# Second SwiGLU layer of an encoder block: weight sums of a Strassen pair formed by adding DMA loads, and one product in another PSUM pool

## Chip, cores and metric

One core of a Trainium2 chip. The metric is the device time of one execution in microseconds; several executions are timed and their median is given.

## The reference

One residual block on x (512 tokens, 1024 features), float32: a half-step SwiGLU layer, a token mixer (gated DeltaNet and latent attention), and a second half-step SwiGLU layer, each behind an adaptive RMS norm. Only the second SwiGLU layer matters here:

```python
def _swiglu(h, w_in, w_out):                    # h 512x1024, w_in 1024x5632, w_out 2816x1024
    gate, up = jnp.split(h @ w_in, 2, axis=-1)
    return (jax.nn.silu(gate) * up) @ w_out
x = x + 0.5 * g3[:, None, :] * _swiglu(_modulate(x, sh3, s3), ffn2_w_in[l], ffn2_w_out[l])
```

## The kernel before

Activations are kept feature-major, in tiles of 128 features by 512 tokens. Each float32 operand is split into a high part (a cast to fp32r on ScalarE) and a low part (a subtract on VectorE), and a product is made of three matmuls: high by high, high by low, low by high.

The 2816 hidden features of the second layer are 22 blocks of 128, each with a gate block `g` and an up block `u` of the weights (1024 rows, loaded as one tile of 128 x 1024, 512 KB). The first four blocks (eight "units", 0 to 7) are multiplied plainly. The other 18 are "pairs": `g` and `u` of one block, each halved along the 1024 rows (A and B), with the tokens halved too, form a 2x2 matrix product that a Strassen scheme computes with seven products instead of eight. It needs four sums of weight halves: gA + gB, uA + gA, and two more made of these. `pair_tasks` makes the sums, splits all weights and handles the results; `product` makes the seven products (`up0`, `up1`, `s2`, `s3`, `s1`, `s4`, `gate1`), each of 12 matmuls of 256 columns. `token_sums` makes the sums on the token side, T(0) to T(7).

**Order.** `ffn2_rest` writes the order of the layer out by hand, and `in_order` pins it: on every engine, and on SyncE's queue of loads, the instructions run in the order in which the program emits them. The loop runs over ticks s; pair j has base 7j, and its products stand at base + 0, 1, 3, 4, 6, 9 and 12 (`STEPS`). The list in `pair_tasks` says at which tick, counted from the base, a task is emitted: the load at -11, the sums at -7 and -5, the splits from -6 to 0, and then the copies, sums and SiLUs of the results. Between the products, `fill` places the matmuls of the down projection (`down`, four blocks at a time, whose weights are cast four ticks and subtracted three ticks before use, and `finish`, line 868, which adds a result tile to x). For ticks 24 to 38 there are almost no fills.

**The entry.** Before tick 0, the list `steps` interleaves units 3 to 7, the token sums, the first SwiGLU results (`glu`) and the tasks of pair 0. An entry that is a generator is run to its first `yield`, and its second half is run after the first half of the next one; a tuple is run at once. Pair 0's tasks at base + 0 and earlier stand in `steps` and not in the tick list. Pair 1's load stands in `steps` and in the tick list as well.

**Buffers.** Raw weights go to pool `wp` with tag `wr`, four buffers of 512 KB, shared by units, pairs and down weights; a load waits until a buffer's last reader is done. High and low parts have four buffers each (`wh`, `wl`). The sums have one buffer each in `ws` (`sx` and `sy`). The two PSUM pools are `psa` (three banks, taken with `acc`) and `psb` (five banks, taken with `aux`). Units 0 to 2 are accumulated in the three banks of `psa` before the entry; products 3 to 7 take their banks in `products`.

In the profile a tile's name is that of its variable or tag: `sx` and `sy` are the sums, `gh`/`gl` the parts of gB, `yh`/`yl` those of the tile `y`, `pa` and `pb` the banks of `psa` and `psb`. GpSimd (POOL) has no work in the second layer.

Of the kernel before, what the change touches and what calls it, by code (L numbers as in the profile page):

```python
# [11 lines left out]
F32 = mybir.dt.float32  # L12
# [3 lines left out]
ALU = mybir.AluOpType  # L16
AX = mybir.AxisListType

P = 128
NT = 512  # L20
# [3 lines left out]
DFF = 2816  # L24
# [55 lines left out]
class Block:  # L80
# [656 lines left out]
    def pair_tasks(self, f, base, add):  # L737


        nc, v, w = self.nc, self.nc.vector, self.ins["ffn2_w_in"][0]  # L740
        r = {}
        flat = lambda t: t.rearrange("p k f -> p (k f)")
        A, B = slice(0, NT), slice(NT, 2 * NT)

        def tiles(names, tags, dt, bufs):
            for n, tag in zip(names, tags):
                r[n] = self.ws.tile([P, 2 * NT], dt, tag=tag, name=self.name(tag), bufs=bufs)

        def load():
            for n, c in (("g", f * P), ("u", DFF + f * P)):  # L750
                t = self.wp.tile([P, 8, P], F32, tag="wr", name=self.name("wr"))
                self.load(t, w[:, c:c + P].rearrange("(k p) f -> p k f", p=P))
                r[n] = flat(t)

        def sums():
            tiles(("x", "y"), ("sx", "sy"), F32, 1)
            v.tensor_tensor(out=r["y"][:, A], in0=r["g"][:, A], in1=r["g"][:, B], op=ALU.add)
            v.tensor_tensor(out=r["x"][:, A], in0=r["u"][:, A], in1=r["g"][:, A], op=ALU.add)

        def sums2():  # L760
            v.scalar_tensor_tensor(out=r["x"][:, B], in0=r["y"][:, A], scalar=-1.0, in1=r["u"][:, A], op0=ALU.mult,
                                   op1=ALU.subtract)
            v.tensor_tensor(out=r["y"][:, B], in0=r["u"][:, B], in1=r["x"][:, B], op=ALU.subtract)

        def hi(name, src, part=slice(0, 2 * NT)):
            def go():
                if name == "g1":
                    r["g1h"], r["g1l"] = self.slot(F32R, "gh"), self.slot(F32R, "gl")
                elif name == "y":
                    tiles(("yh", "yl"), ("yh", "yl"), F32R, 2)  # L770
                else:
                    for e in "hl":
                        r[name + e] = flat(self.wp.tile([P, 8, P], F32R, tag="w" + e, name=self.name("w" + e)))
                nc.scalar.copy(r[name + "h"], r[src][:, part])
            return go

        def lo(name, src, part=slice(0, 2 * NT)):
            def go():
                v.tensor_tensor(out=r[name + "l"], in0=r[src][:, part], in1=r[name + "h"].bitcast(F32), op=ALU.subtract)
            return go  # L780

        def early_copy(name, part):
            def go():
                if name not in r:
                    r[name] = self.slot(s=name)
                nc.scalar.copy(r[name][:, part], r["A"][:, :HALF])
            return go

        L, H = slice(0, HALF), slice(HALF, NT)

        def both():
            v.tensor_tensor(out=r["cc"], in0=r["cc"], in1=r["BC"], op=ALU.add)

        def gate0():
            v.tensor_tensor(out=r["uc"][:, H], in0=r["uc"][:, L], in1=r["BC"][:, H], op=ALU.add)
            nc.scalar.activation(r["uc"][:, H], r["uc"][:, H], AF.Silu, scale=-1.0)

        def gate1():
            nc.scalar.activation(r["cc"][:, H], r["cc"][:, H], AF.Silu, scale=-1.0)

        def act1():
            v.tensor_tensor(out=r["cc"][:, H], in0=r["cc"][:, H], in1=r["A"][:, :HALF], op=ALU.mult)

        def act0():
            v.tensor_tensor(out=r["cc"][:, L], in0=r["cc"][:, L], in1=r["uc"][:, H], op=ALU.mult)
            r["ah"] = self.slot(F32R, "ah")
            nc.scalar.copy(r["ah"], r["cc"])

        def act_low():
            al = self.slot(F32R, "al")  # L810
            v.tensor_tensor(out=al, in0=r["cc"], in1=r["ah"].bitcast(F32), op=ALU.subtract)
            self.act.append((r["ah"], al))

        r["do"] = dict(load=load, sums=sums, sums2=sums2)
        for n, src, part in (("u", "u", slice(0, 2 * NT)), ("x", "x", slice(0, 2 * NT)), ("y", "y", slice(0, 2 * NT)), ("g1", "g", B)):
            r["do"][n] = hi(n, src, part), lo(n, src, part)
        for at, go in ((-11, load), (-7, sums), (-5, sums2), (-6, hi("u", "u")), (-4, lo("u", "u")), (-4, hi("x", "x")),
                       (-3, lo("x", "x")), (-3, hi("y", "y")), (-2, lo("y", "y")), (-1, hi("g1", "g", B)),
                       (0, lo("g1", "g", B)), (1, early_copy("cc", L)), (4, early_copy("uc", L)), (7, early_copy("cc", H)),
                       (8, both), (9, gate1), (11, act1), (13, gate0), (15, act0), (16, act_low)):  # L820
            if base > 0 or at > 0:
                add(base + at, go)
        return r

    def product(self, r, what):


        if "A" not in r:
            r["A"], r["BC"] = self.aux(), self.aux()
        L, H = slice(0, HALF), slice(HALF, NT)  # L830
        b = lambda k0, ts: [(self.h[k][0][:, ts], self.h[k][1][:, ts]) for k in range(k0, k0 + 4)]
        out, w, part, xs, start, stop = {
            "up0": (r["A"][:, L], "u", 0, b(0, L), True, False), "up1": (r["BC"][:, L], "u", 1, b(4, L), True, True),
            "s2": (r["A"][:, L], "x", 1, self.T["t2"], False, False), "s3": (r["BC"][:, H], "x", 0, self.T["t3"], True, False),
            "s1": (r["A"][:, L], "y", 0, self.T["t1"], False, False), "s4": (r["A"][:, L], "y", 1, b(4, H), False, True),
            "gate1": (r["BC"][:, H], "g1", 0, self.T["t4"], False, True)}[what]
        mm, kw = self.nc.tensor.matmul, dict(skip_group_check=True)
        for k, (xh, xl) in enumerate(xs):
            c = slice(part * NT + k * P, part * NT + k * P + P)
            wh, wl = r[w + "h"][:, c], r[w + "l"][:, c]  # L840
            mm(out, wh, xh, start=start and k == 0, stop=False, **kw)  # L841
            mm(out, wh, xl, start=False, stop=False, **kw)  # L842
            mm(out, wl, xh, start=False, stop=stop and k == 3, **kw)  # L843

    def ffn2_rest(self, ps):

        nc = self.nc
# [10 lines left out]
        n = FT - PLAIN  # L858
# [50 lines left out]
        d0 = down(0, 4, 1, 1.3)  # L909
# [12 lines left out]
        raws, split, accs = {}, {3: self.next_unit(ahead=0)}, {0: ps[0], 1: ps[1], 2: ps[2]}  # L922

        def unit_split(i):
            hi, lo = (self.wp.tile([P, 8, P], F32R, tag=t, name=self.name(t)) for t in ("wh", "wl"))
            nc.scalar.copy(hi, raws[i])
            split[i] = hi, lo
            yield
            nc.vector.tensor_tensor(out=lo, in0=raws[i], in1=hi.bitcast(F32), op=ALU.subtract)  # L929

        def glu(f):
            s = self.slot(s="sg")
            nc.scalar.activation(s, accs[2 * f], AF.Silu)
            a = self.slot(s="af")
            nc.vector.tensor_tensor(out=a, in0=s, in1=accs[2 * f + 1], op=ALU.mult)
            ah, al = self.slot(F32R, "ah"), self.slot(F32R, "al")
            nc.scalar.copy(ah, a)
            self.act.append((ah, al))
            yield
            nc.vector.tensor_tensor(out=al, in0=a, in1=ah.bitcast(F32), op=ALU.subtract)  # L940

        def products(i):
            accs[i] = self.acc()
            self.dense(accs[i], split[i], self.h)

        def of(go):
            if isinstance(go, tuple):
                go[0]()
                yield
                go[1]()  # L950
            else:
                go()
# [2 lines left out]
        T = lambda i: self.token_sums(i % 4, i // 4)  # L955
        for i in (4, 5, 6, 7):
            raws[i] = raw(i)
        steps = [unit_split(4), T(0), T(1), glu(0), (products, 3), T(2), (do["load"],), unit_split(5), T(3), (products, 4),
                 glu(1), T(4), unit_split(6), T(5), (products, 5), of(do["sums"]), of(do["sums2"]), unit_split(7), (d0[0],),
                 glu(2), (products, 6), T(6), of(do["u"]), of(do["x"]), (do1["load"],), T(7), of(do["y"]), of(tuple(d0[1:])),  # L960
                 (products, 7), glu(3), of(do["g1"])]
        waiting = None
        for g in steps:
            if isinstance(g, tuple):
# [8 lines left out]
        k0, m = 16, 6  # L973
# [1127 lines left out]
```

## Time and profile before

| | us |
|---|---|
| timed executions | 1081.54, 1086.86, 1089.51 (median 1086.86) |
| profiled execution, whole | 1081.86 |
| its span in the trace | 1080.1 |
| PE busy in the span | 1046.8 (97%) |
| VectorE busy | 698.7 (65%) |
| ScalarE busy | 436.8 (40%) |
| GpSimd busy | 43.3 (4%) |
| first matmul of product 3 (entry) | 739.77 |
| first matmul of pair 0 | 768.71 |

The trace's times count from the start of the span, and 1.8 us of the execution lie around it. A row of the timeline has start, duration, engine, line, operation, the tile written and the tiles read, shape, count, and in brackets how long the engine was idle before it and what released it. PE's rows overlap, since matmuls are pipelined; the distance from one start to the next is the time that each takes.

### The profile page before, as it was taken

To read this page: it belongs to the slowest core of one execution; us is meant where nothing else is said; L and a number is where in the kernel's file an instruction comes from. 1 tells how busy PE (TensorE), PEld (TensorE's weight loads), DVE (VectorE), ACT (ScalarE), POOL (GpSimd) and SP (SyncE) were. 2 spreads that over 40 slices of the span, in tenths; PEclk is the share of its full clock that TensorE was granted. 3 is DMA by queue.
4 is the path that set the end of the run, shared out by engine and by line. 5 is a ranking of instruction groups with operands and counts; after the bars stand their busy time and mean duration, and the time that the engine had idled before them with its cause. 6 is when DMAs were issued, how large, how long until landed. Compare 5 with 4: busy or idle time off the path is not lost. (4 is left out here: it accounts for less than half of the span.)

```text
span 1080.1 us, 15643 instructions
## 1 busy us (share of the span) xinstructions
PE 1046.8 (97%) x6183; PEld 897.7 (83%) x6183; DVE 698.7 (65%) x1240; ACT 436.8 (40%) x752; POOL 43.3 (4%) x94
## 2 busy tenths in 40 slices
PE   6999999999999999998999899998999999999998
PEld 4778878788887899886777678987899999999997
DVE  4488984333587456468867645787768877777633
ACT  4242222222222345475574443454434444444322
POOL 1000000000000010102000030200000000000000
PEclk9999999999999999999999889999999999999999
DMA  9989973332687345211213001121532433333222
GB/s 274 274 250 299 288 217 98 98 98 88 212 289 235 108 127 165 76 39 40 79 34 89 20 21 40 39 79 59 156 116 74 123 104 99 93 117 98 65 73 78
DMA packets 204471, 133.18 MB, mean 123 GB/s; under 512 B 13665, under 2 KB 188526, under 8 KB 204398
## 3 DMA queue, kind: packets, MB, share of 16 engines
q1 hardware_dynamic: 204398, 132.18, 41.4%
q8 instruction: 48, 0.79, 0.3%
q14 instruction: 25, 0.20, 0.1%
HBM read 129.67 MB, written 2.49 MB: 122 GB/s over the span
## 5 line engine op out<-in xcount | busy, mean ns | idle before, releaser
L262 PE MATMUL pa<-hh,wh 128*128 128x512 f32 (+1 forms) x605 | 230.5, 381 | 8.4 <-ACT z L1916 4.3
L263 PE MATMUL pa<-hl,wh 128*128 128x512 f32 (+1 forms) x605 | 228.6, 378 | 3.5 <-DVE hl L449 3.3
L264 PE MATMUL pa<-hh,wl 128*128 128x512 f32 (+1 forms) x605 | 227.8, 377 | 0.0
L193 ACT CAST wh<-wr 128x1024 fp32r<-128x1024 f32 (+1 forms) x106 | 107.7, 1018 | 253.9 <-PE pa L263 177.6
L194 DVE TENSOR_TENSOR wl<-wr,wh 128x1024 fp32r<-128x1024 f32 (+1 forms) x106 | 125.1, 1181 | 101.9 <-ACT wh L193 99.5
L262 PE MATMUL pa<-ah,wh 128*128 128x512 f32 (+1 forms) x396 | 145.5, 367 | 0.5 <-DVE xT L868 0.4
L263 PE MATMUL pa<-al,wh 128*128 128x512 f32 (+1 forms) x396 | 144.5, 365 | 0.0
L264 PE MATMUL pa<-ah,wl 128*128 128x512 f32 (+1 forms) x396 | 143.5, 362 | 0.0
L262 PEld LDWEIGHTS pa<-hh,wh 128*128 128x128 f32 x605 | 114.6, 190 | 32.7 <-ACT z L1916 4.7
L263 PEld LDWEIGHTS pa<-hl,wh 128*128 128x128 f32 x605 | 114.6, 189 | 24.1 <-DVE hl L449 4.8
L264 PEld LDWEIGHTS pa<-hh,wl 128*128 128x128 f32 x605 | 114.7, 190 | 20.2 <-DVE wl L194 0.4
L264 PEld LDWEIGHTS pa<-ah,wl 128*128 128x128 f32 x396 | 74.8, 189 | 12.0
L262 PEld LDWEIGHTS pa<-ah,wh 128*128 128x128 f32 x396 | 75.2, 190 | 10.4 <-ACT wh L193 1.7
L547 DVE SCALAR_TENSOR_TENSOR aa<-ar,sc,aa 128x512 f32<-128x512 f32 x98 | 73.0, 748 | 13.1 <-DMA ar<-in_w_ada 11.6
L263 PEld LDWEIGHTS pa<-al,wh 128*128 128x128 f32 x396 | 75.2, 190 | 7.2
L841 PE MATMUL pb<-fh,wh 128*128 128x256 f32 x144 | 40.7, 283 | 0.0
L868 DVE SCALAR_TENSOR_TENSOR xT<-pa,mod,xT 128x512 f32<-128x512 f32 (+1 forms) x40 | 29.4, 736 | 17.6 <-PE pa L264 17.6
L843 PE MATMUL pb<-fh,wl 128*128 128x256 f32 x144 | 40.7, 283 | 0.0
L843 PE MATMUL pb<-hh,wl 128*128 128x256 f32 x144 | 40.7, 283 | 0.0
L842 PE MATMUL pb<-fl,wh 128*128 128x256 f32 x144 | 40.7, 282 | 0.0
L842 PE MATMUL pb<-hl,wh 128*128 128x256 f32 x144 | 40.7, 282 | 0.0
L841 PE MATMUL pb<-hh,wh 128*128 128x256 f32 x144 | 40.6, 282 | 0.0
(430 smaller groups left out, 1956.5 us busy)
## 6 DMA issues: line engine op xcount, KB each, us to landing
wr<-in_ffn_w_in SPq DMA_DIRECT2D x84, 512.0 KB, 3.9
ar<-in_w_ada SPq DMA_DIRECT2D x48, 512.0 KB, 6.9
wr<-in_ffn_w_out SPq DMA_DIRECT2D x34, 512.0 KB, 4.1
ar<-in_w_ada SPq DMA_DIRECT2D x48, 256.0 KB, 4.2
wr<-in_w_in SPq DMA_DIRECT2D x21, 512.0 KB, 3.9
wr<-in_ffn_w_out SPq DMA_DIRECT2D x17, 384.0 KB, 3.5
wr<-in_w_out SPq DMA_DIRECT2D x8, 512.0 KB, 4.6
wr<-in_ffn_w_in SPq DMA_DIRECT2D x8, 384.0 KB, 7.2
```

The source lines that it names most:

```text
L193: self.nc.scalar.copy(hi, raw)
L194: self.nc.vector.tensor_tensor(out=lo, in0=raw, in1=hi.bitcast(F32), op=ALU.subtract)
L262: mm(out, wh, xh, start=start, stop=False)
L263: mm(out, wh, xl, start=False, stop=False)
L264: mm(out, wl, xh, start=False, stop=stop)
L547: nc.vector.scalar_tensor_tensor(out=acc, in0=a, scalar=sc, in1=acc, op0=ALU.mult, op1=ALU.add)
L841: mm(out, wh, xh, start=start and k == 0, stop=False, **kw)
L842: mm(out, wh, xl, start=False, stop=False, **kw)
L843: mm(out, wl, xh, start=False, stop=stop and k == 3, **kw)
L868: nc.vector.scalar_tensor_tensor(out=self.xT[t][:, ts], in0=p[:, ts], scalar=gate[:, t:t + 1], in1=self.xT[t][:, ts], op0=ALU.mult, op1=AL ...
```

## The change

Two of the four weight sums of each pair are no longer made on VectorE. Before, `sums` made gA + gB in `y` and uA + gA in `x` with two VectorE instructions. Now SyncE loads uA a second time into `x`, and GpSimd issues two loads with `accum_op=ALU.add`: gA is added to `x`, and gB is added to the A half of `g`, which then holds gA + gB beside gB and takes the place of `y`. The fourth sum, in `sums3`, overwrites uA in the tile `u`. So the tile `sy` is gone and `sx` has two buffers; products `s4` and `gate1` swap which split weights they read; the load moves to tick -10, the sums to -9, and the other tasks by a tick or so. `x` and `u` are split from their tiles as before, `y` from `g`, and `g1` from the A half of `u`.

In the entry, product 3 takes its bank from `psb` (`aux`) instead of `psa`, T(0) to T(2) stand ahead of the split of unit 4, and the tasks of pairs 0 and 1 are placed anew. Pair 1's first two tasks are left out of the tick list, so that its load is emitted once.

```diff
@@ -746,21 +746,27 @@
             for n, tag in zip(names, tags):
                 r[n] = self.ws.tile([P, 2 * NT], dt, tag=tag, name=self.name(tag), bufs=bufs)
 
+        rows = lambda c, k0, n: w[k0 * P:(k0 + n) * P, c:c + P].rearrange("(k p) f -> p k f", p=P)
+        cg, cu = f * P, DFF + f * P
+
         def load():
-            for n, c in (("g", f * P), ("u", DFF + f * P)):
+            tiles(("x",), ("sx",), F32, 2)
+            for n, c in (("g", cg), ("u", cu)):
                 t = self.wp.tile([P, 8, P], F32, tag="wr", name=self.name("wr"))
-                self.load(t, w[:, c:c + P].rearrange("(k p) f -> p k f", p=P))
+                self.load(t, rows(c, 0, 8))
                 r[n] = flat(t)
+            self.load(r["x"][:, A].rearrange("p (k f) -> p k f", k=4), rows(cu, 0, 4))
 
         def sums():
-            tiles(("x", "y"), ("sx", "sy"), F32, 1)
-            v.tensor_tensor(out=r["y"][:, A], in0=r["g"][:, A], in1=r["g"][:, B], op=ALU.add)
-            v.tensor_tensor(out=r["x"][:, A], in0=r["u"][:, A], in1=r["g"][:, A], op=ALU.add)
+            for n, k0 in (("x", 0), ("g", 4)):
+                nc.gpsimd.dma_start(r[n][:, A].rearrange("p (k f) -> p k f", k=4), rows(cg, k0, 4), accum_op=ALU.add)
 
         def sums2():
-            v.scalar_tensor_tensor(out=r["x"][:, B], in0=r["y"][:, A], scalar=-1.0, in1=r["u"][:, A], op0=ALU.mult,
+            v.scalar_tensor_tensor(out=r["x"][:, B], in0=r["g"][:, A], scalar=-1.0, in1=r["u"][:, A], op0=ALU.mult,
                                    op1=ALU.subtract)
-            v.tensor_tensor(out=r["y"][:, B], in0=r["u"][:, B], in1=r["x"][:, B], op=ALU.subtract)
+
+        def sums3():
+            v.tensor_tensor(out=r["u"][:, A], in0=r["u"][:, B], in1=r["x"][:, B], op=ALU.subtract)
 
         def hi(name, src, part=slice(0, 2 * NT)):
             def go():
@@ -811,14 +817,15 @@
             v.tensor_tensor(out=al, in0=r["cc"], in1=r["ah"].bitcast(F32), op=ALU.subtract)
             self.act.append((r["ah"], al))
 
-        r["do"] = dict(load=load, sums=sums, sums2=sums2)
-        for n, src, part in (("u", "u", slice(0, 2 * NT)), ("x", "x", slice(0, 2 * NT)), ("y", "y", slice(0, 2 * NT)), ("g1", "g", B)):
+        r["do"] = dict(load=load, sums=sums, sums2=sums2, sums3=sums3)
+        for n, src, part in (("u", "u", slice(0, 2 * NT)), ("x", "x", slice(0, 2 * NT)), ("y", "g", slice(0, 2 * NT)), ("g1", "u", A)):
             r["do"][n] = hi(n, src, part), lo(n, src, part)
-        for at, go in ((-11, load), (-7, sums), (-5, sums2), (-6, hi("u", "u")), (-4, lo("u", "u")), (-4, hi("x", "x")),
-                       (-3, lo("x", "x")), (-3, hi("y", "y")), (-2, lo("y", "y")), (-1, hi("g1", "g", B)),
-                       (0, lo("g1", "g", B)), (1, early_copy("cc", L)), (4, early_copy("uc", L)), (7, early_copy("cc", H)),
-                       (8, both), (9, gate1), (11, act1), (13, gate0), (15, act0), (16, act_low)):
-            if base > 0 or at > 0:
+        for i, (at, go) in enumerate(((-10, load), (-9, sums), (-5, hi("u", "u")), (-4, lo("u", "u")), (-4, sums2), (-3, hi("x", "x")), (-3, sums3),
+                       (-2, lo("x", "x")), (-1, hi("y", "g")), (0, lo("y", "g")), (0, hi("g1", "u", A)),
+                       (1, lo("g1", "u", A)), (1, early_copy("cc", L)), (4, early_copy("uc", L)), (7, early_copy("cc", H)),
+                       (8, both), (9, gate1), (11, act1), (13, gate0), (15, act0), (16, act_low))):
+            by_hand = 12 if base == 0 else 2 if base == 7 else 0
+            if i >= by_hand:
                 add(base + at, go)
         return r
 
@@ -832,8 +839,8 @@
         out, w, part, xs, start, stop = {
             "up0": (r["A"][:, L], "u", 0, b(0, L), True, False), "up1": (r["BC"][:, L], "u", 1, b(4, L), True, True),
             "s2": (r["A"][:, L], "x", 1, self.T["t2"], False, False), "s3": (r["BC"][:, H], "x", 0, self.T["t3"], True, False),
-            "s1": (r["A"][:, L], "y", 0, self.T["t1"], False, False), "s4": (r["A"][:, L], "y", 1, b(4, H), False, True),
-            "gate1": (r["BC"][:, H], "g1", 0, self.T["t4"], False, True)}[what]
+            "s1": (r["A"][:, L], "y", 0, self.T["t1"], False, False), "s4": (r["A"][:, L], "g1", 0, b(4, H), False, True),
+            "gate1": (r["BC"][:, H], "y", 1, self.T["t4"], False, True)}[what]
         mm, kw = self.nc.tensor.matmul, dict(skip_group_check=True)
         for k, (xh, xl) in enumerate(xs):
             c = slice(part * NT + k * P, part * NT + k * P + P)
@@ -940,7 +947,7 @@
             nc.vector.tensor_tensor(out=al, in0=a, in1=ah.bitcast(F32), op=ALU.subtract)
 
         def products(i):
-            accs[i] = self.acc()
+            accs[i] = self.aux() if i == 3 else self.acc()
             self.dense(accs[i], split[i], self.h)
 
         def of(go):
@@ -955,10 +962,10 @@
         T = lambda i: self.token_sums(i % 4, i // 4)
         for i in (4, 5, 6, 7):
             raws[i] = raw(i)
-        steps = [unit_split(4), T(0), T(1), glu(0), (products, 3), T(2), (do["load"],), unit_split(5), T(3), (products, 4),
-                 glu(1), T(4), unit_split(6), T(5), (products, 5), of(do["sums"]), of(do["sums2"]), unit_split(7), (d0[0],),
-                 glu(2), (products, 6), T(6), of(do["u"]), of(do["x"]), (do1["load"],), T(7), of(do["y"]), of(tuple(d0[1:])),
-                 (products, 7), glu(3), of(do["g1"])]
+        steps = [T(0), T(1), T(2), unit_split(4), glu(0), (products, 3), T(3), unit_split(5), (do["load"],), (do["sums"],), (products, 4), T(4),
+                 glu(1), unit_split(6), T(5), (products, 5), unit_split(7), (d0[0],), of(do["sums2"]), T(6),
+                 of(do["u"]), glu(2), of(do["sums3"]), (products, 6), of(do["x"]), (do1["load"],), (do1["sums"],), T(7), of(do["y"]),
+                 of(tuple(d0[1:])), (products, 7), glu(3), of(do["g1"])]
         waiting = None
         for g in steps:
             if isinstance(g, tuple):
```

## Prediction

> **What bounds the kernel now.** I read the page's busy shares first, then busy time by stage over the second FFN, then the PE timeline around the one hole that the stages show, then VectorE, ScalarE and SyncE over one steady pair.
>
> ```profile
> PE 1046.8 (97%) x6183; PEld 897.7 (83%) x6183; DVE 698.7 (65%) x1240; ACT 436.8 (40%) x752; POOL 43.3 (4%) x94
> 736.00:740.00 4.00, 0.34 (x2) 0.23 (x2) 2.90 (x5) 2.03 (x4) 0.00 (x0) 1.00 0.23 68
> 740.00:744.00 4.00, 4.00 (x12) 3.13 (x12) 3.84 (x8) 2.19 (x3) 0.00 (x0) 0.57 0.21 63
> 744.00:764.00 20.00, 20.00 (x90) 16.55 (x89) 15.22 (x25) 8.53 (x12) 0.00 (x0) 1.00 0.27 80
> 838.00:1040.00 202.00, 201.96 (x1404) 188.52 (x1403) 146.31 (x203) 87.00 (x144) 0.00 (x0) 1.00 0.34 100
> ```
>
> The columns after the stretch are its length, busy time (and count) of PE, PEld, DVE, ACT and POOL, granted clock, DMA share and GB/s. In the loop over pairs (838 to 1040) PE is busy 201.96 of 202 us, DVE 146.31 and POOL not at all. So VectorE work taken away there is worth nothing by itself: PE's matmuls hide it. The hole is the entry, 736 to 740, and the stretch behind it runs at a granted clock of 0.57.
>
> ```profile
> 735.83 0.28 PE L264 MATMUL pa<-hh,wl 128*128 128x256 f32 x1
> 739.77 0.57 PE L262 MATMUL pa<-hh,wh 128*128 128x512 f32 x1 [3.66 <-ACT sg L933]
> 740.13 0.63 PE L263 MATMUL pa<-hl,wh 128*128 128x512 f32 x1
> 750.35 0.39 PE L262 MATMUL pa<-hh,wh 128*128 128x512 f32 x1
> 750.58 0.39 PE L263 MATMUL pa<-hl,wh 128*128 128x512 f32 x1
> 738.60 0.62 ACT L733 CAST fh<-tv 128x512 fp32r<-128x512 f32 x1 [1.68 <-DVE tv L723]
> 739.12 0.59 ACT L933 ACTIVATE sg<-pa 128x512 f32<-128x512 f32 x1
> ```
>
> Product 3, the fourth unit, has to wait for a bank of the three in pool `psa`: all three hold units 0 to 2, and the first is free when SiLU `sg` has read it (739.12). ScalarE comes to it late because it first casts token sums that VectorE makes. PE stands for 3.66 us. Its next matmuls start about 0.43 us apart (12 in the 4 us row above) instead of the 0.23 us of 750.35 to 750.58.
>
> **The change part by part.**
>
> *The bank.* Product 3 goes to the other pool, whose last entry tile was read before 736, so it follows at once: 3.66 us gained. With no stop I take the slow stretch as gone too: nine spacings of 0.43 instead of 0.23, less the ramp at both ends, 1.7 us. Sum of the entry: -5.4 us (bounds -3.7 if the slow clock comes anyway, -5.4). Moving T(0) to T(2) ahead of the fourth unit's split costs nothing: it is VectorE work pulled into the 2.90-of-4 us row's time, in which VectorE waited for `wh` before.
>
> *VectorE.* Two sums per pair leave (0.68 us each, rows below at 898.20 and 898.80), 18 pairs, 24.5 us of busy time: worth 0 under a PE that is full. Without that cover they would be worth those 1.36 us a pair.
>
> *SyncE and the bytes.* Each pair adds a third load of 256 KB and two adding loads of 256 KB from GpSimd: 18 x 0.75 MB. Two 512 KB loads go: pair 1 is loaded twice before, by the entry and by tick -4, and the change skips the second.
>
> ```profile
> 759.99 8.54 SPq L118 DMA_DIRECT2D wr<-in_ffn_w_in  x4
> 764.02 0.99 SPq L118 DMA_DIRECT2D wr<-in_ffn_w_in  x2
> 898.31 0.37 SPq L118 DMA_DIRECT2D wr<-in_ffn_w_out  x1
> 900.65 4.55 SPq L118 DMA_DIRECT2D wr<-in_ffn_w_in  x2
> wr<-in_ffn_w_in SPq DMA_DIRECT2D x84, 512.0 KB, 3.9
> ar<-in_w_ada SPq DMA_DIRECT2D x48, 256.0 KB, 4.2
> ```
>
> Four issues of `in_ffn_w_in` stand between 759.99 and 768.53 where two would do. The DMA share of 0.34 in the loop stays well below 1 at 1.75 times a pair's bytes, so bandwidth costs 0.
>
> *The waits: where the price lies.* The sums now end in DMA. VectorE's `sums2` waits for the second adding load, and everything behind it on VectorE waits along: `sums3`, the low parts of `x`, `y` and `g1`, the end of a product (L802, L795) and `finish` (L868), which free banks for PE. So the question is when that load lands.
>
> Its start hangs on the four `wr` buffers. Before, `u` was free four ticks ahead of its pair's first product; now `u` is overwritten by `sums3` and read until `lo("g1")` at tick 1, and `g` until `lo("y")` at 0, while the loads come at -10. Between ticks -3 and 0 two pairs hold all four buffers, and a `down` weight wants one as well. In SyncE's fixed order (down, g, u, x) the down load takes the first free buffer, `g` the second, and `u` with `x` behind it has to wait until `lo("y")` of the pair before has ended. That is tick -7 of its pair, not -10. In the trace of before a load already issues the moment such a subtract ends: the second issue of the 900.65 row is at its end less 0.37, 904.83, and the subtract at 903.59 below ends at 904.81. So each pair now closes a ring: `lo("y")`, load `u`, load `x`, two adding loads, `sums2`, VectorE work, `lo("y")`.
>
> ```profile
> 838.24 0.28 PE L841 MATMUL pb<-hh,wh 128*128 128x256 f32 x1
> 852.06 0.28 PE L841 MATMUL pb<-hh,wh 128*128 128x256 f32 x1
> 898.80 0.28 PE L841 MATMUL pb<-hh,wh 128*128 128x256 f32 x1
> 914.38 0.28 PE L841 MATMUL pb<-hh,wh 128*128 128x256 f32 x1
> 918.64 0.28 PE L841 MATMUL pb<-hh,yh 128*128 128x256 f32 x1
> 977.39 0.28 PE L841 MATMUL pb<-hh,wh 128*128 128x256 f32 x1
> 993.67 0.28 PE L841 MATMUL pb<-hh,wh 128*128 128x256 f32 x1
> 898.20 0.68 DVE L757 TENSOR_TENSOR sy<-wr 128x512 f32<-128x512 f32 x1
> 898.80 0.69 DVE L758 TENSOR_TENSOR sx<-wr,wr 128x512 f32<-128x512 f32 x1
> 902.26 0.68 DVE L761 SCALAR_TENSOR_TENSOR sx<-sy,wr 128x512 f32<-128x512 f32 x1
> 903.59 1.22 DVE L779 TENSOR_TENSOR wl<-wr,wh 128x1024 fp32r<-128x1024 f32 x1
> 905.38 0.75 DVE L868 SCALAR_TENSOR_TENSOR xT<-pa,mod,xT 128x512 f32<-128x512 f32 x1 [0.58 <-PE pa L264]
> 906.05 0.41 DVE L802 TENSOR_TENSOR cc<-cc,pb 128x256 f32<-128x256 f32 x1
> 908.17 1.22 DVE L779 TENSOR_TENSOR yl<-sy,yh 128x1024 fp32r<-128x1024 f32 x1 [0.57 <-ACT yh L774]
> 911.76 0.42 DVE L795 TENSOR_TENSOR uc<-uc,pb 128x256 f32<-128x256 f32 x1 [2.37 <-PE pb L843]
> 907.08 1.05 ACT L774 CAST yh<-sy 128x1024 fp32r<-128x1024 f32 x1
> 912.22 0.42 ACT L796 ACTIVATE uc<-uc 128x256 f32<-128x256 f32 x1 [4.08 <-DVE uc L795]
> 913.05 1.04 ACT L898 CAST wh<-wr 128x1024 fp32r<-128x1024 f32 x1
> 914.00 0.37 ACT L786 COPY cc<-pb 128x256 f32<-128x256 f32 x1
> ```
>
> The ring, from the end of one `lo("y")`: `x` is issued 0.06 + 0.62 us later (start of one load to the next in the 764.02 row: 0.99 less 0.37) and lands in 4.2, together 4.9. Then A, the time of both adding loads. Then, start to start, `sums2` 0.60, finish 0.66, L802 0.33, `sums3` 0.60, low of `x` 1.14, L795 0.33, finish 0.66, low of `y` 1.22: 5.5. The ring takes 10.4 + A. PE takes 15.58 us per pair (898.80 to 914.38) and 16.28 in the last ones (977.39 to 993.67). Up to A = 5.2 PE sets the pace; above it VectorE falls behind by A - 5.2 per pair.
>
> There is some room. The seven ticks before pair 6 have almost no down work (838.24 to 852.06, 13.82 us), and the two finishes drop out of the ring: 9.1 + A, so pair 6 starts out A - 4.7 late. PE feels it when product `s4`, 19.84 us after its pair's first matmul (898.80 to 918.64), lacks the ScalarE copy L786. That copy stands behind the cast of `y` and the down cast, 6.6 us after `sums2` (3.75 us of VectorE up to the end of L795, then 0.42, 1.05, 1.04 and 0.37 overlapped): 4.9 + A + 6.6 against 19.84 leaves 8.3 - A. With about seven pairs at 15.58 and three at 16.28 the loop loses (A - 4.7) + 7(A - 5.2) + 3(A - 5.9) - (8.3 - A) = 12A - 67.1 us, and nothing below A = 5.6.
>
> *A itself* is shown nowhere: POOL issues no load before. Bound from below: two 256 KB loads that overlap wholly, 4.2 us (the `ar` row). From above: one after the other, 8.4, since GpSimd takes its two issues in order and the second cannot start before `x` has landed and the first is prepared. The second load surely overlaps the first partly, and nothing brings it nearer to one end, so I take the middle, 6.3.
>
> The Trainium skill, DMA: Bandwidth & Descriptors, section on the anatomy of a GpSimd-issued DMA, fits 2.0 us plus bytes over 436 GB/s for each such load; an estimate by that page is 2.6 us each, 5.2 for two in line, by which the loop would lose nothing and the time be about 1077.5. No run here shows it, and the row of 256 KB says 4.2.
>
> *The entry's own ring.* `sums2` of pair 0 now stands on VectorE before the low part of unit 7 and the second last token sum. `u` of pair 0 gets the buffer of unit 5:
>
> ```profile
> 744.05 1.22 DVE L929 TENSOR_TENSOR wl<-wr,wh 128x1024 fp32r<-128x1024 f32 x1
> ```
>
> This subtract ends at 745.3 before and, without the hole, some 2 us earlier: `x` lands near 748.3, `sums2` starts at 748.3 + A, and the SiLU that frees product 7's bank ends some 5.3 us later (0.60, 1.14 and 0.8 of VectorE, then casts of 0.62 and 1.05 and a SiLU of 0.59, with the gaps between). Product 7 is due at 736.1 + 4 x 24 x 0.227 = 757.9. Stall A - 4.2: 2.1 us for 6.3, and 0 to 4.2 over the bounds.
>
> *Sum.* 1081.86 (profiled execution) - 5.4 + 2.1 + (12 x 6.3 - 67.1 = 8.5) = 1087.1. The four times of before (1081.54, 1081.86, 1086.86, 1089.51) average 3.0 above the profiled one, and their median of the timed three is 5.0 above; with the 3.0 the forecast is 1090.
>
> **The rivals.**
>
> *Hidden.* A at or below 5.2: only the entry counts, 1076.5 to 1077.5 (net -5.4 to -4.4). For it: POOL has nothing else to do, and DMA share is 0.34. Against: the 256 KB row alone takes 4.2, and there are two in line.
>
> *Serial, the other side.* GpSimd prepares and the chip adds one load after the other, A = 8.4. The place is `sums2` on VectorE, the point from which it decides is A = 6.7, the price 12 x 8.4 - 67.1 = 33.7 in the loop and 4.2 in the entry: 1114.4. For it: 512 separate rows of 512 B per load, each read, read again at its target, and written. Against: two engine-side steps of different loads may overlap.
>
> *Held up by VectorE.* GpSimd's preparation waits out the VectorE instruction in progress, up to 1.22 us for each load: A = 6.3 + 2.4 = 8.7, net +36.4, 1118.3. Against: the loop's VectorE rows all run at the same rate per column (0.68 us for 512, 1.22 for 1024). The Trainium skill, SBUF — State Buffer, section Who interferes with whom, tells of such a hold-up while VectorE runs a two-port mode, and advises issuing from SP or ACT; by its list two-input operations like these have no such mode, and the equal rates agree.
>
> *The bank isn't free.* If product 3 waits on in the other pool, the entry keeps its 5.4: 1092.5 with the forecast's loop. Against: nothing in the entry holds that pool after 736.
>
> **How the numbers follow.** Forecast, A between 5.2 and 6.7 (net -4.4 to +10): 0.34, its own range 1080 to 1095. Hidden 0.16, bank not free 0.03: with the forecast they are "within 1%", 0.53. One per cent, 10.8 us, is about what a measurement of this kernel can tell from no change. Serial 0.33 and held up 0.10 are "slower", 0.43. For "faster by over 1%" no row offers 10.8 us: 0.04. The range reaches from the hidden case on the profiled execution's side, 1077, to the serial case on the median's, 1119; beyond it lie part of the held-up case and what no row shows.
>
> **What would show it.** Right: no idle before product 3 and a granted clock of 1.00 behind it; POOL's two issues right behind each landing of `x`; `u` loads that start as a low part of `y` ends; VectorE idle before L761 with a DMA as releaser, 3 to 5 us a pair; PE idle of about 1 us a pair from pair 7 on. Wrong: no idle at L761 (A is small), PE idle of 3 us and more a pair (serial), `u` issued at tick -10 (the buffer ring doesn't exist), or a hole that merely moved to products 4 to 7.

## The result and the profile after

The changed kernel takes 1122.15 us (median of 4, 1119.42 to 1126.24) against 1088.18 for the kernel before (median of 4): ratio 1.0337, 95% interval 1.0298 to 1.0377. It is 3.4% slower; the forecast was 1090, within 1% of the kernel before, and the range ended at 1119.

Different executions reach the second FFN up to some 9 us apart, and this has nothing to do with the change. So the stages are compared from the last matmul of its norm (L437) on, read off PE's timeline:

| | entry: last L437 to pair 0 | loop: pair 0's first matmul to the last pair's last | to the end |
|---|---|---|---|
| before | 44.5 | 278.6 | 32.9 |
| after | 43.6 | 317.1 | 32.9 |

The whole loss, 38.5 us between these two profiled executions, lies in the loop over pairs; the entry gained 0.9 us. (The medians differ by 34.0 us.) The busy times of the changed kernel by stage (columns as in the prediction) show the same:

```profile
740.00:764.00 24.00, 22.48 (x102) 18.37 (x101) 13.54 (x22) 8.61 (x13) 2.80 (x2) 1.00 0.45 103
764.00:772.00 8.00, 6.54 (x23) 5.33 (x24) 7.21 (x10) 5.56 (x8) 0.00 (x0) 0.79 0.19 56
772.00:838.00 66.00, 66.00 (x463) 61.81 (x462) 42.30 (x57) 27.87 (x47) 12.91 (x10) 1.00 0.74 160
838.00:1060.00 222.00, 199.56 (x1309) 179.30 (x1308) 120.39 (x166) 80.39 (x133) 31.17 (x24) 0.97 0.59 131
```

PE was busy 201.96 of 202 us from 838 on; now it is 199.56 of 222. VectorE does less work and is still not the bound by its busy time. Who waits is told by the view of waits, VectorE first, then PE (total, times, longest):

```profile
DVE sx L765 <- DMA wr<-in_ffn_w_in: 94.3, 17, 8.4
DVE wl L785 <- ACT wh L780: 22.8, 18, 3.0
PE pb L848 <- ACT cc L792: 20.5, 14, 2.3
PE pa L262 <- ACT sg L940: 3.0, 1, 3.0
PE pb L848 <- DVE cc L808: 1.9, 2, 1.2
PE pa L264 <- DVE wl L994: 1.9, 1, 1.9
```

L765 is `sums2`, and it waits for the load that adds to `g` (the tile has the tag `wr`). PE waits for the ScalarE copy that had line 786 before and has 792 now. In the entry it waits for the SiLU that frees product 7's bank. The other three waits of PE lie in the loop and add up to 24.3 us, less than the loop's 38.5: after some of the stops PE also runs at a slow clock (rows in the last section), which takes some 6 us more, and the rest is not broken down. One steady pair, by VectorE, SyncE and GpSimd:

```profile
902.46 1.23 DVE L785 TENSOR_TENSOR yl<-wr,yh 128x1024 fp32r<-128x1024 f32 x1 [0.76 <-ACT yh L780]
909.32 1.23 DVE L785 TENSOR_TENSOR wl<-wr,wh 128x1024 fp32r<-128x1024 f32 x1 [2.36 <-ACT wh L780]
916.23 0.69 DVE L765 SCALAR_TENSOR_TENSOR sx<-wr,wr 128x512 f32<-128x512 f32 x1 [5.69 <-DMA wr<-in_ffn_w_in]
916.84 0.74 DVE L875 SCALAR_TENSOR_TENSOR xT<-pa,mod,xT 128x512 f32<-128x512 f32 x1
917.50 0.41 DVE L808 TENSOR_TENSOR cc<-cc,pb 128x256 f32<-128x256 f32 x1
917.83 0.69 DVE L769 TENSOR_TENSOR wr<-wr,sx 128x512 f32<-128x512 f32 x1
918.43 1.22 DVE L785 TENSOR_TENSOR wl<-sx,wh 128x1024 fp32r<-128x1024 f32 x1
919.57 0.41 DVE L801 TENSOR_TENSOR uc<-uc,pb 128x256 f32<-128x256 f32 x1
919.90 0.74 DVE L875 SCALAR_TENSOR_TENSOR xT<-pa,mod,xT 128x512 f32<-128x512 f32 x1
921.41 1.23 DVE L785 TENSOR_TENSOR yl<-wr,yh 128x1024 fp32r<-128x1024 f32 x1 [0.76 <-ACT yh L780]
```

```profile
903.72 0.37 SPq L118 DMA_DIRECT2D wr<-in_ffn_w_in  x1
904.18 0.53 SPq L118 DMA_DIRECT2D sx<-in_ffn_w_in  x1
904.85 0.41 SPq L118 DMA_DIRECT2D wr<-in_ffn_w_out  x1
```

```profile
909.49 1.28 POOL L762 DMA_DIRECT2D sx<-in_ffn_w_in  x1 [16.40 <-DMA sx<-in_ffn_w_in]
910.24 1.84 POOL L762 DMA_DIRECT2D wr<-in_ffn_w_in  x1
```

The median times from issue to landing, for `x` and for the two adding loads of a pair:

```profile
sx<-in_ffn_w_in SPq DMA_DIRECT2D x18, 256.0 KB, 4.4
sx<-in_ffn_w_in POOLq DMA_DIRECT2D x18, 256.0 KB, 4.8
wr<-in_ffn_w_in POOLq DMA_DIRECT2D x18, 256.0 KB, 6.0
```

This is the ring. The low part of `y` ends at 903.69, and `u` is issued at 903.72: it did wait for that buffer. `x` follows at 904.18 and has landed when GpSimd starts at 909.49. The second adding load ends VectorE's wait at 916.23, and the next low part of `y` ends at 922.64. One turn takes 922.64 - 903.69 = 18.95 us, where PE needs 15.58: 5.8 us of loads, 6.7 of adding loads (the prediction's A), 6.4 from `sums2` to the end of the ring. This turn is typical: the ten turns between the low parts of `y` that end at 846.70 and at 1035.21 last 18.85 us on average, from 18.2 to 19.9.

### The profile page after: what moved, and what is told of

It reads as the page before. It is cut to its first block, busy times and chain, and to the rows that moved or that the text cites. A ratio compares the mean times of both kernels' runs of the same rounds, so it can differ in the third digit from the quotient of the medians.

```text
span 1122.4 us, 15787 instructions
## 1 busy us (share of the span) xinstructions
PE 1064.2 (95%) x6183; PEld 905.2 (81%) x6183; DVE 673.2 (60%) x1204; ACT 435.4 (39%) x752; POOL 90.2 (8%) x130
## 3 DMA queue, kind: packets, MB, share of 16 engines
q0 software_dynamic: 19008, 9.44, 6.9%
## 5 line engine op out<-in xcount | busy, mean ns | idle before, releaser
L262 PE MATMUL pa<-hh,wh 128*128 128x512 f32 (+1 forms) x597 | 228.1, 382 | 7.6 <-ACT z L1923 4.3
L263 PE MATMUL pa<-hl,wh 128*128 128x512 f32 (+1 forms) x597 | 225.7, 378 | 3.2 <-DVE hl L449 3.1
L264 PE MATMUL pa<-hh,wl 128*128 128x512 f32 (+1 forms) x597 | 225.2, 377 | 0.0
L765 DVE SCALAR_TENSOR_TENSOR sx<-wr,wr 128x512 f32<-128x512 f32 x18 | 12.5, 692 | 94.3 <-DMA wr<-in_ffn_w_in 94.3
L780 ACT CAST wh<-sx 128x1024 fp32r<-128x1024 f32 x18 | 18.9, 1051 | 104.8 <-DVE sx L765 99.6
L762 POOL DMA_DIRECT2D sx<-in_ffn_w_in x18 | 23.3, 1292 | 283.6 <-DMA sx<-in_ffn_w_in 224.8
L848 PE MATMUL pb<-fh,wh 128*128 128x256 f32 x144 | 43.0, 299 | 1.0 <-ACT cc L792 0.5
```

Source lines behind the costliest of these rows:

```text
L262: mm(out, wh, xh, start=start, stop=False)
L263: mm(out, wh, xl, start=False, stop=False)
L264: mm(out, wl, xh, start=False, stop=stop)
L762: nc.gpsimd.dma_start(r[n][:, A].rearrange("p (k f) -> p k f", k=4), rows(cg, k0, 4), accum_op=ALU.add)
L765: v.scalar_tensor_tensor(out=r["x"][:, B], in0=r["g"][:, A], scalar=-1.0, in1=r["u"][:, A], op0=ALU.mult, op1=ALU.subtract)
```

## The experiments

Two theories were put against each other. *Ring*: the chain above sets the pace, and whatever takes one link out gives PE its pace back. *Bandwidth*: the added bytes and the dearer packets of the adding loads fill the DMA engines, and everything lands late. Ratios are against the kernel before, in the same job; entry and loop are cut as in the table above.

| kernel | median us | ratio (95%) | entry | loop |
|---|---|---|---|---|
| after | 1122.15 | 1.0337 (1.0298 to 1.0377) | 43.6 | 317.1 |
| e1_bank | 1079.68 | 0.9954 (0.9935 to 0.9972) | 39.0 | 278.6 |
| e2_swap | 1082.13 | 0.9965 (0.9945 to 0.9985) | 39.0 | 280.5 |
| e3_five | 1081.10 | 0.9961 (0.9949 to 0.9974) | 39.0 | 278.3 |
| e4_plain | 1097.20 | 1.0113 (1.0093 to 1.0133) | 39.7 | 293.2 |
| e5_vec | 1081.89 | 0.9967 (0.9949 to 0.9984) | 39.0 | 279.4 |
| e6_free | 1089.68 | 1.0033 (1.0018 to 1.0048) | 43.4 | 281.9 |
| e7_psa | 1080.86 | 0.9943 (0.9925 to 0.9962) | 40.1 | 278.3 |
| e8_once | 1080.81 | 0.9942 (0.9915 to 0.9969) | 39.0 | 278.6 |

**The bank alone (e1_bank).** In the kernel before:

```diff
         def products(i):
-            accs[i] = self.acc()
+            accs[i] = self.aux() if i == 3 else self.acc()
```

> The kernel before, with product 3's bank taken from the other pool and nothing else changed. If the hole before product 3 is only the wait for a bank, PE goes on at once: 3.7 us of idle time and 1.7 us of slow clock are gained, about 5.4 us against the kernel before. Rival: the hole moves to product 4, whose weights are split late, and the gain is under 2 us.

The entry falls from 44.5 to 39.0 us, the loop stays at 278.6. Stages of e1_bank around product 3:

```profile
735.00:743.00 8.00, 8.00 (x54) 7.35 (x53) 3.19 (x6) 2.67 (x4) 0.00 (x0) 1.00 0.09 25
743.00:767.00 24.00, 24.00 (x110) 19.95 (x109) 22.78 (x36) 13.76 (x20) 0.00 (x0) 1.00 0.38 113
```

PE is full, at a granted clock of 1.00. The hole didn't move: neither idle time nor slow clock is left, and together they were worth 5.5 us, as forecast.

**The order of the two adding loads (e2_swap).** In the changed kernel:

```diff
-            for n, k0 in (("x", 0), ("g", 4)):
+            for n, k0 in (("g", 4), ("x", 0)):
```

> The changed kernel, with GpSimd issuing the load that adds to g first and the one that adds to x second. Ring theory (lo of y, loads of u and x, adding loads, sums2, VectorE work, lo of y): sums2 needs only g, whose plain load lands long before, so the wait at L765 goes and the ring falls from 18.95 us to 15.3 to 15.8 a pair, near PE's 15.58: about 1085 to 1092 us instead of 1122. Rival (the adding loads' packets fill the DMA engines and everything lands late): nothing changes, 1115 to 1125.

One line brings 1122 back to 1082, with the same bytes, packets and operations. That is 3 us under the expected range: the entry falls to 39.0 us as well, so the stall before product 7 is gone too, which the expectation doesn't name. GpSimd and VectorE of e2_swap in a steady pair, and a stage of the loop:

```profile
877.30 1.28 POOL L762 DMA_DIRECT2D sx<-in_ffn_w_in  x1 [10.91 <-DMA sx<-in_ffn_w_in]
881.33 1.28 POOL L762 DMA_DIRECT2D wr<-in_ffn_w_in  x1 [2.75 <-DMA wr<-in_ffn_w_in]
```

```profile
877.11 1.23 DVE L785 TENSOR_TENSOR wl<-wr,wh 128x1024 fp32r<-128x1024 f32 x1 [2.07 <-ACT wh L780]
878.25 0.69 DVE L765 SCALAR_TENSOR_TENSOR sx<-wr,wr 128x512 f32<-128x512 f32 x1
883.22 1.23 DVE L785 TENSOR_TENSOR wl<-sx,wh 128x1024 fp32r<-128x1024 f32 x1 [2.70 <-ACT wh L780]
```

```profile
838.00:1040.00 202.00, 201.57 (x1388) 185.76 (x1388) 128.48 (x178) 86.03 (x144) 29.55 (x23) 1.00 0.67 150
```

In the changed kernel the load that adds to `g` stands behind the one that adds to `x` on GpSimd, and so waits for `x` to land although `g` landed long before. Here it is issued for the next pair at 881.33, before `x` of that pair has landed (GpSimd's next issue, at 892.89, follows that landing), so `sums2` runs without a wait behind the low part of `u`. What is left of the adding loads in the ring is the one into `x`, before its cast. The turns now last 15.5 to 16.5 us, about PE's own 15.58, and the loop is 1.9 us longer than before the change. The bandwidth theory falls here.

**A fifth raw buffer (e3_five).** In the changed kernel, at every tile of tag `wr`, and with two general slots fewer to make room:

```diff
-        self.slots = ctx.enter_context(tc.tile_pool(name="slots", bufs=56))
+        self.slots = ctx.enter_context(tc.tile_pool(name="slots", bufs=54))
...
-                t = self.wp.tile([P, 8, P], F32, tag="wr", name=self.name("wr"))
+                t = self.wp.tile([P, 8, P], F32, tag="wr", name=self.name("wr"), bufs=5)
```

> The changed kernel with five buffers for raw weights instead of four (and 54 general slots instead of 56). Ring theory: u no longer waits for the lo of y of the pair before, so it is loaded three ticks (6.7 us) earlier, more than the 3.4 us by which the ring is too long: the loop runs at PE's pace, about 1085 to 1092 us. Rival (bandwidth): the same bytes and packets, no change, 1115 to 1125.

Loop 278.3. The time, 1081.1, is 4 us under the expected range, and here too the entry falls to 39.0. A stage of e3_five in the loop:

```profile
838.00:1040.00 202.00, 202.00 (x1405) 188.71 (x1404) 132.06 (x180) 87.57 (x146) 30.90 (x24) 1.00 0.67 148
```

The DMA share, 0.67, is higher than the 0.59 of the changed kernel, and PE is full. The adding loads themselves cost nothing as soon as `u` starts early enough.

**Plain instead of adding (e4_plain).** In the changed kernel:

```diff
-                nc.gpsimd.dma_start(r[n][:, A].rearrange("p (k f) -> p k f", k=4), rows(cg, k0, 4), accum_op=ALU.add)
+                nc.gpsimd.dma_start(r[n][:, A].rearrange("p (k f) -> p k f", k=4), rows(cg, k0, 4))
```

> The changed kernel with the two GpSimd loads as plain loads that overwrite their target instead of adding (so two weight sums are not formed). It gives the price of adding beside that of loading from GpSimd. Ring theory: A, the time from the landing of x to the landing of the second of them, falls from 6.8 us to about 4.7 if a packet takes 31 ns as from SyncE instead of 65; ring 16.8, loss about 1.2 us a pair: 1095 to 1103. If GpSimd's issuing is the price and not the adding, A stays over 6 and the time over 1112.

GpSimd and VectorE of e4_plain in a steady pair:

```profile
879.35 0.75 POOL L762 DMA_DIRECT2D sx<-in_ffn_w_in  x1 [14.87 <-DMA sx<-in_ffn_w_in]
880.08 0.75 POOL L762 DMA_DIRECT2D wr<-in_ffn_w_in  x1
884.33 0.69 DVE L765 SCALAR_TENSOR_TENSOR sx<-wr,wr 128x512 f32<-128x512 f32 x1 [4.03 <-DMA wr<-in_ffn_w_in]
```

A is 884.33 - 879.35 = 5.0 in this turn. Over nine steady turns it is 4.4 to 6.0, 5.3 on average, where the changed kernel has 6.4 to 8.1, 6.9 on average. The loop loses 14.6 us instead of 38.5. So adding, rather than loading, makes some 1.6 us of A, and 23.9 us of the loss: about 15 us of loop for each us of A, where the forecast had 12. But two plain loads from GpSimd in this place would be too slow as well.

**The sums on VectorE, all else as changed (e5_vec).**

```diff
         def sums2():
+            tiles(("x",), ("sx",), F32, 2)
+            v.tensor_tensor(out=r["x"][:, A], in0=r["u"][:, A], in1=r["g"][:, A], op=ALU.add)
+            v.tensor_tensor(out=r["g"][:, A], in0=r["g"][:, A], in1=r["g"][:, B], op=ALU.add)
```

and the third load and the adding loads are left out.

> The changed kernel with the two sums back on VectorE, in place and at the tick of sums2, and without the third load and the adding loads; the new buffer holds, the entry and the bank stay. Ring theory: only the adding loads make the ring too long; without A (6.8 us) and with 1.4 us of VectorE work instead, and u alone to wait for, it is some 12 us, under PE's 15.58: 1078 to 1086 us. Rival (the longer hold of u's buffer alone is the price): still over 1100.

1081.9 us, loop 279.4. The longer hold of `u` and the later ticks are harmless by themselves; it takes both, the late load and the adding loads behind it.

**`u` freed early (e6_free).**

```diff
-            v.tensor_tensor(out=r["u"][:, A], in0=r["u"][:, B], in1=r["x"][:, B], op=ALU.subtract)
+            r["s"] = self.slot(s="us")
+            v.tensor_tensor(out=r["s"], in0=r["u"][:, B], in1=r["x"][:, B], op=ALU.subtract)
```

with `g1` split from `r["s"]`.

> The changed kernel with the result of sums3 in a general slot instead of in u's own tile, so that u's raw buffer is free at tick -3 instead of 1; four raw buffers, adding loads as they are. Ring theory: the loop's ring now runs from sums3 to sums3: loads 5.7, A 6.8, then 2.3 of VectorE, 14.8 a pair, under PE's 15.58, so the loop's loss goes; the entry's stall before product 7 (3 us and the slow clock behind it) stays: 1083 to 1092 us. Rival (bandwidth, or the adding loads themselves): 1110 to 1125.

Waits of e6_free, VectorE and PE:

```profile
DVE sx L765 <- DMA wr<-in_ffn_w_in: 71.1, 16, 8.0
PE pa L262 <- ACT sg L941: 2.5, 1, 2.5
```

The loop is back at 281.9 although VectorE still waits 71.1 us at `sums2`: a wait of the engine that isn't the bound costs little when its ring is about as long as PE's. The ring is longer than expected, though: its steady turns last 15.4 to 16.7 us and not 14.8, since A is 8.0 to 9.1 here and not 6.8 (why is not shown), and the loop is still 3.3 us longer than before the change. What is left beside that is the entry, 43.4: the stall before product 7 (2.5 us) and the slow clock behind it (0.79 from 764 to 772) are there as in the changed kernel.

**Product 3 back in the first pool (e7_psa),** in e3_five:

```diff
-            accs[i] = self.aux() if i == 3 else self.acc()
+            accs[i] = self.acc()
```

> The changed kernel with five raw buffers, and product 3 back in the first pool. With T(0) to T(2) ahead the SiLU that frees the bank already comes about 1 us after product 2's end, so the bank itself is worth about 1 us here and not 5.4: a hole of some 1 us before product 3, no slow clock behind it, 1081 to 1084 us. Rival: the hole of 3.7 us and the slow clock are back, 1086 or more.

The hole before product 3, in e7_psa:

```profile
736.31 0.28 PE L264 MATMUL pa<-hh,wl 128*128 128x256 f32 x1
737.43 0.50 PE L262 MATMUL pa<-hh,wh 128*128 128x512 f32 x1 [0.84 <-ACT sg L940]
```

0.84 us, and an entry of 40.1 instead of 39.0. So with the new order of the token sums the first pool costs only 1.1 us, where it cost 5.5 with the old one: bank and order are two cures for one fault. The order alone, in the kernel before, was not run.

**Pair 1's load once (e8_once),** in e1_bank:

```diff
-            if base > 0 or at > 0:
+            if at > 0 or (base > 0 and not (base == 7 and go is load)):
```

> The kernel before with product 3's bank from the other pool and pair 1's second load left out. PE is full from the entry to the end, so leaving out 1 MB of loads is worth nothing: the same as the bank alone, 5 us under the kernel before. Rival: the second load delayed others, 2 us or more are gained on top.

Entry and loop are those of e1_bank to 0.1 us: the second load cost nothing. Of all kernels run, e1_bank, e2_swap, e3_five, e5_vec, e7_psa and e8_once are faster than the kernel before, by 0.3 to 0.6%. Their intervals stay below 1 and overlap. The adding loads add nothing to what the entry gives.

## Why the prediction was wrong

*The bound and the entry's hole*: right. -5.4 was forecast for the bank, and the entry of e1_bank shows -5.5, with neither idle time nor slow clock left.

*VectorE's relief is worth 0; bytes and the double load are worth 0*: right (e5_vec, e3_five, e8_once).

*The ring*: right in every link, the buffer, `sums2` as the place, and L786 as the copy that PE misses. Each experiment that took out a link brought the loop back, to between 278.3 and 281.9 us.

*The ring's terms*: here it failed. Forecast were 4.9 + 6.3 + 5.5 = 16.7 us a turn, measured 5.8 + 6.7 + 6.4 = 18.95. All three were too short:

- The loads, by 0.9: I let `x` land 4.2 us after its issue at 0.68 and GpSimd start at once. It took 5.3 from 904.18 to GpSimd's start: 4.8 to the landing (4.4 is the median of all pairs), and some 0.55 from the landing to GpSimd's start, a term that the sum didn't have.
- The adding loads, by 0.4. That the middle of the bounds (4.2 and 8.4) came near was luck, since no row stood behind it. The second load is issued 0.75 us after the first, so the two overlap almost wholly, but it then takes 6.0 us to land and not 4.2; together 6.75. Adding makes some 1.6 us of it (e4_plain).
- VectorE, by 0.9: I added VectorE's instructions alone. In the trace the low part of `y` stands 0.76 us idle for ScalarE's cast, which waits in turn for the SiLU behind L801. The cast was counted for PE's copy, but not for the ring.

With these terms the prediction's own formula gives 12 x (6.7 + 1.8) - 67.1 = 34.9 us for the loop, against 38.5 measured. The slope of 12 us per us is what made the small errors matter: 0.4 to 0.9 us in a chain, ten to twelve times over. The other 3.6 us are not broken down, but the room that the formula allows ahead of the loss was smaller than forecast: PE's first stop in the loop, 1.75 us up to 846.71, stands before `s4` of pair 4, where PE was to stand from pair 7 on. The idle time before L765 is larger than forecast as well: 5.4 to 7.2 us a pair in most turns instead of 3 to 5.

*The entry's ring*: right in kind, product 7 waits for its bank behind `sums2`, and mis-sized: 2.1 us forecast, 3.0 measured. The slow clock behind the new stall (0.79 in the row 764 to 772) was left out of the sum, though the row 740 to 744 of before had shown it. So the entry gave 0.9 us and not 3.3.

*The rivals*: on the profiled execution's base the held-up case (net +36.4) and the serial case (+32.5) are nearer to the measured +37.6 than the forecast (+5.2), but only in size and by luck: both need A above 8, and it is 6.7. Of GpSimd being held up by VectorE nothing is seen: in e2_swap one issue runs beside VectorE's low part of `u` (877.30) and one in VectorE's idle time (881.33), and both last 1.28 us. In the serial case the second load would start when the first has landed; it is issued 0.75 us behind it.

## What to carry to other kernels

When work moves from an engine to a load, look for the ring that closes through the buffers: from the load's wait for a free buffer, over everything in order behind its landing, back to the read that frees the buffer. Compare its length with the bound engine's period, and count every engine in it, waits between them too; each microsecond over is paid once per turn. If a ring is too long, first reorder so that the load that is ready early goes first: here one swapped pair of issues was worth 40 us.

## What the runs showed of the hardware

An adding load is dear in packets. Here are the queue lines (packets, MB, share of 16 engines) of the changed kernel from 725 to 1122 us, and of e4_plain from 725 to 1100. The queue q0 holds GpSimd's loads, q1 the transfers of SyncE.

```profile
q1 hardware_dynamic: 66944, 37.75, 33.0%
q0 software_dynamic: 19008, 9.44, 19.5%
```

```profile
q0 software_dynamic: 2880, 9.44, 8.7%
```

The adding loads move 9.44 MB in 19008 packets at 19.5% of 16 engines over 397 us, 65 ns a packet of some 500 B, while SyncE's transfers take 31 ns a packet of some 560 B. The same bytes loaded plainly from GpSimd need only 2880 packets, and the adding loads keep the DMA engines busy 2.4 times as long (19.5% of 397 us against 8.7% of 375). GpSimd's rows of the issues last 0.75 us when plain, and 1.28 and 1.84 when adding; the second issue starts 0.75 us after the first in both kernels.

The clock after a stop isn't a matter of the stop's length alone: after two stops of PE of 2.28 us each in the changed kernel, which end at 885.03 and at 903.70, the granted clock was 1.00 once and 0.65 once. Three more stretches behind stops, shown with them, had a slow clock.

```profile
846.70:851.00 4.30, 4.29 (x23) 4.29 (x24) 3.27 (x5) 2.04 (x5) 0.00 (x0) 0.60 0.71 182
885.00:889.00 4.00, 3.93 (x28) 3.46 (x29) 3.29 (x6) 1.71 (x4) 0.00 (x0) 1.00 0.71 196
903.70:907.70 4.00, 4.00 (x20) 3.71 (x21) 3.26 (x5) 1.68 (x4) 0.00 (x0) 0.65 0.63 169
942.00:946.00 4.00, 3.93 (x17) 3.65 (x18) 3.33 (x6) 1.74 (x5) 0.00 (x0) 0.57 0.73 200
979.00:983.00 4.00, 3.76 (x17) 3.47 (x18) 3.50 (x6) 1.92 (x5) 0.00 (x0) 0.62 0.62 176
```

The slow clock didn't set the loop's pace. The four turns of the ring that begin with these slow stretches last 18.4 to 18.9 us, the other six of the ten 18.2 to 19.9; PE only has less left to wait for: its stop at the end of such a turn lasts 1.3 to 1.8 us, where the four other turns up to 979.24 end with 2.1 to 3.5 us of stops.
